# The start and the last rows of a two-layer mixer trunk: norm weight by a product with ones, another order of the first loads, splits in runs of 256, a tile apart for the last scaling

## The chip, the cores and the metric

The kernel runs on one core of a Trainium2 chip. The metric is the device time of one execution, in microseconds (us). A profile of one execution stands beside the times; its engines are called PE (TensorE, the matrix unit; PEld is its weight load), DVE (VectorE), ACT (ScalarE), POOL (GpSimd) and SP (SyncE, which here only issues DMAs).

## What is computed

256 tokens of width 1024 in float32 go through two residual layers and a last RMSNorm. The reference, cut to its frame:

```python
for layer in range(DEPTH):                       # 2
    h = rms_norm(x, norm_w[layer])               # x (1, 256, 1024)
    proj = jnp.einsum('bsd,de->bse', h, w_in[layer])     # 1024 -> 12832 columns
    ...                                          # three token mixers: SSD, sliding window, forgetting attention
    branch = jnp.einsum('bsiw,iwd->bsid', ys, w_proj[layer])
    g = jax.nn.sigmoid(gates.reshape(b, s, N_BRANCH, d) + gate_bias[layer])
    merged = jnp.sum(g * branch, axis=2)
    x = x + jnp.einsum('bsd,de->bse', merged, w_out[layer])
return rms_norm(x, final_norm_w)
```

`rms_norm` divides a row by the root of its mean square (plus 1e-6) and multiplies by a weight of 1024 entries.

## The kernel before

The tokens lie on 128 partitions in two tiles, t = 0 and t = 1. Every dense product is computed in three passes from float32 numbers split in a high and a low part of PE's fast format (`fp32r`): high by high, low by high, high by low. `split` (L261) makes both parts: ACT copies (`hi`), DVE subtracts (`lo`). A weight matrix comes in pieces; a piece is cut in parts of 512 KB, 128 by 1024, which SP loads (`load_to`, L332, six `raw` buffers), and which `feed` (L363) splits as soon as fewer than four split parts are held. `release` (L377) gives parts back and calls `feed`.

The work is a list `ops` of units: a unit is one piece by one token tile (or by one run of channels). `dense` (L278) writes the 24 matmuls of a unit: eight blocks `k` of 128 of the width, three passes each. PE's order is the list's own for the whole kernel; small jobs (transposes, attention, scan) are put between units by a clock of the program's own (`launch`, `pump`). Behind the start only PE's order is written out; the orders of the other engines are planned by the tile framework. In the start (L1139 to L1186) DVE, ACT and POOL, too, run in the order in which the program writes their instructions. Every engine runs its own in that order, and an instruction that waits holds all behind it.

The start, in words:

- SP loads x's tile 0, then the norm weight spread over 128 partitions (512 KB, `nwb`), then x's tile 1 (L161 to L163), then the weight parts.
- PE runs 30 transposes of the identity (`WARM`, L1142) that no one reads.
- For tile 0 (L1159 to L1165): squares summed, half by DVE and half by ACT; the inverse root by a power on POOL and four small DVE steps (`rsqrt`, L200); DVE scales x by root and weight in two halves of 512 columns into `h[0]`.
- `to_hT` (L270) turns four blocks of 128 by 128 on PE into one PSUM buffer, and splits the buffer at one go, 512 columns, into `hTh` and `hTl`.
- For tile 1 POOL multiplies by the weight and ACT by the root (L1167 to L1181).
- The generator `shared` (L1148) splits a weight part in halves: ACT both high halves, DVE one low half and POOL the other. It is used for parts 0 and 1 (the first piece, keys of the window attention) and for parts 2 and 3 (the second piece, its values).
- The first two units are that first piece by tile 0 and by tile 1 (`u_bkv`, L475). The first has a special order: `dense` with `after` takes blocks 0 to 3 in three passes, then blocks 4 to 7, and calls a function after every 12 matmuls (L289): `second_rows`, which turns a half of tile 1 and splits a further part.
- A unit of keys ends with `rope`: three DVE instructions on the unit's PSUM buffer (L470 to L473), then two POOL adds (L492). They stand right behind the unit in DVE's order.
- `release` at L1185 lets `feed` split the next parts; the third unit is the second piece by tile 0.

The end of the last layer, `out_end` (L993), for each tile: DVE adds the residual into `y.xn` (L996); ACT sums its squares (L997); DVE multiplies `y.xn` by -0.5 and the final weight, in place (L1001); from the sum the inverse root; DVE and ACT scale a half each (L1011, L1013) and the two halves are stored. `L8` is a tag of eight buffers of 128 by 2048 that are taken in turn.

PSUM has two kinds of buffer here: three `mm` for units, five `mx` (`pmx`) for the rest.

Of the kernel before, what the change touches and what calls it, by code (L numbers as in the profile page):

```python
# [16 lines left out]
P = 128  # L17
# [11 lines left out]
T_PP, T_SSD, T_BIAS = 1, 1, 1  # L29
N_RAW, N_SPLIT = 6, 6  # L30
AHEAD = 4
WARM = 30
VERBOSE = False


# [8 lines left out]
def hybrid_trunk(  # L44
# [53 lines left out]
    def transpose(o, a, i):  # L98
        clock["t"] += 0.109
        nc.tensor.transpose(o, a, i)  # L100
# [58 lines left out]
    x0 = T("L8", [P, 2, D])  # L159
    nwb0 = T("nwb", [P, D])  # L160
    nc.sync.dma_start(x0[:, 0, :], x2[0:P, :])  # L161
# [3 lines left out]
    make_identity(nc, ident)  # L165
    tri = T("tri", [P, P])
    nc.gpsimd.memset(tri, 1.0)
    nc.gpsimd.affine_select(out=tri, in_=tri, compare_op=ALU.is_ge, fill=0.0, base=0,
# [7 lines left out]
    ones = T("ones", [P, P])  # L176
    nc.gpsimd.memset(ones, 1.0)

    wmask = T("wmask", [P, 2 * P])
    nc.gpsimd.memset(wmask, 0.0)  # L180
# [97 lines left out]
    def dense(pt, ah, al, bh, bl, w, after=None, mid=None):  # L278


        passes = ((ah, bh), (al, bh), (ah, bl))
        if after is None:
            seq = [(k, a, b) for k in range(NK) for a, b in passes]
        else:
            seq = [(k, a, b) for k0 in (0, 4) for a, b in passes for k in range(k0, k0 + 4)]
        for i, (k, a, b) in enumerate(seq):
            mm(pt, a(k), b(k), start=(i == 0), stop=(i == len(seq) - 1))
            if after is not None:
                if i % 12 == 11:  # L289
# [111 lines left out]
        y.l = l  # L401
        layers.append(y)
    y0 = layers[0]
    y0.nwb = nwb0

    pdma = pin(nc.scalar.dma_start)

# [585 lines left out]
    def out_end(y, c, t, i, n, xo, p):  # L993
        sl = slice(c, c + n)
        with tc.high_priority():
            tt(halves(y.xn[:, t, sl]), p, halves(xo), op=ALU.add)  # L996
            sum_sq(y.xn, t, c, y.ss[t][:, i:i + 1], n)  # L997
            last = y.l + 1 == L
            nwb = fin["w"] if last else layers[y.l + 1].nwb
            if last:  # L1000
                stt(y.xn[:, t, sl], y.xn[:, t, sl], -0.5, nwb[:, sl], op0=ALU.mult, op1=ALU.mult)  # L1001
            else:
                nc.scalar.dma_start(xres[t * P:(t + 1) * P, sl], y.xn[:, t, sl])
            if i == 1:
                y.var[t] = row_var(y.ss[t], 2)
            if i == 2:
                v = y.var[t][:, 1:2]
                stt(v, y.ss[t][:, 2:3], 1.0 / D, y.var[t][:, 0:1], op0=ALU.mult, op1=ALU.add)
                r = row_rsqrt2(v)
                if last:  # L1010
                    ts(y.xn[:, t, 0:512], y.xn[:, t, 0:512], r[:, 0:1], None, op0=ALU.mult)  # L1011
                    nc.sync.dma_start(out2[t * P:(t + 1) * P, 0:512], y.xn[:, t, 0:512])
                    act(y.xn[:, t, 512:D], y.xn[:, t, 512:D], AF.Copy, scale=r[:, 0:1])  # L1013
                    nc.scalar.dma_start(out2[t * P:(t + 1) * P, 512:D], y.xn[:, t, 512:D])
# [30 lines left out]
    def op(i, *fs):  # L1045
        for f in fs:
            ops.append((i, f))

    for y in layers:
# [32 lines left out]

        if l == 0:
            k, v = cols(C_BK), cols(C_BV)
            op(k, u_bkv(y, 0, 0, [lambda j=j: second_rows(j) for j in range(2)]))
# [51 lines left out]

    ENG = mybir.EngineType
    with tc.manual_schedule(engines={ENG.PE, ENG.DVE, ENG.Activation, ENG.Pool}):  # L1139
        load_to(N_RAW)  # L1140
        warm = pmx()
        for i in range(WARM):  # L1142
            transpose(warm[:, 0:P], ident, ident)
        ss = [T("ss", [P, 4], bufs=4) for _ in range(2)]
        h = [T("L4", [P, D]) for _ in range(2)]
        y0.hTh = T("L8", [P, NK // 2, 2, 2 * P], F32R)
        y0.hTl = T("L8", [P, NK // 2, 2, 2 * P], F32R)
        def shared():  # L1148
            for _ in range(2):
                raw, hi, lo = new_part()  # L1150
                for k, sub_ in ((0, tt), (2, gtt)):
                    ks = slice(k, k + 2)
                    act(hi[:, ks, :], raw[:, ks, :], AF.Copy)  # L1153
                    sub_(lo[:, ks, :], raw[:, ks, :], hi[:, ks, :].bitcast(F32), op=ALU.subtract)  # L1154
                yield
        w0, w1 = shared(), shared()
        half = (slice(0, 512), slice(512, D))
        junk = T("L2", [P, 512])
        nc.vector.tensor_tensor_reduce(out=junk, in0=x0[:, 0, half[1]], in1=x0[:, 0, half[1]], scale=1.0,  # L1159
                                       scalar=0.0, op0=ALU.mult, op1=ALU.add, accum_out=ss[0][:, 1:2])  # L1160
        sum_sq(x0, 0, 0, ss[0][:, 0:1], 512)
        r0 = row_rstd(ss[0], 2)
        sum_sq(x0, 1, 0, ss[1][:, 0:1], 512)
        for sl in half:
            stt(h[0][:, sl], x0[:, 0, sl], r0[:, 0:1], y0.nwb[:, sl], op0=ALU.mult, op1=ALU.mult)  # L1165
        sum_sq(x0, 1, 512, ss[1][:, 1:2], 512)
        gtt(h[1][:, half[0]], x0[:, 1, half[0]], y0.nwb[:, half[0]], op=ALU.mult)  # L1167
        v1 = row_var(ss[1], 2)
        to_hT(h[0], 0, y0.hTh, y0.hTl, (0,))
        r1 = rsqrt(v1, 1)  # L1170
        next(w0)
        to_hT(h[0], 0, y0.hTh, y0.hTl, (1,))
        gtt(h[1][:, half[1]], x0[:, 1, half[1]], y0.nwb[:, half[1]], op=ALU.mult)
        def second_rows(j):
            with tc.high_priority():
                to_hT(h[1], 1, y0.hTh, y0.hTl, (j,))
            next(w1)

        act(h[1][:, half[0]], h[1][:, half[0]], AF.Copy, scale=r1[:, 0:1])
        next(w0)  # L1180
        act(h[1][:, half[1]], h[1][:, half[1]], AF.Copy, scale=r1[:, 0:1])  # L1181
        for i, f, _ in ops[:2]:
            f(pieces[i])
        pieces[0].last = True
        release(pieces[0], 2)  # L1185
        run_op(*ops[2])  # L1186
    with tc.manual_schedule(engines={ENG.PE}):
        for i, f, last in ops[3:]:
# [33 lines left out]
```

## Time and profile before

| | us |
|---|---|
| median of 3 runs | 849.24 |
| the runs | 850.91, 849.24, 848.19 |
| span of the profiled execution | 846.0 |
| PE busy in it | 833.7 |
| DVE, ACT, POOL busy | 642.3, 511.6, 105.7 |
| first weight matmul starts | 10.67 |
| third unit starts | 20.22 |
| last matmul starts | 838.84 |

The profiled execution is known by its span alone, from the first instruction to the last; the runs' times hold what lies around it as well.

How to read the profile: a row of the timeline has the start from the span's start, the time that the instruction or a merged group took, the engine, the line of the program, the operation, what it writes and reads, the shape and the count, and in brackets how long the engine stood idle before and whose end it waited for. Groups have the busy time and the mean of one in ns. A group of matmuls in plain float32 holds two records for each product in the program. Lists of waits give the sum in us, how often, and the longest.

### The profile page before, as it was taken

The page shows a single profiled execution, that of the slowest core. Times are in us where ns is not written, and L with a number is a line of the kernel's source. Part 1 is how long each engine was busy: PE and PEld are TensorE (multiplying, and loading weights), DVE is VectorE, ACT ScalarE, POOL GpSimd, SP SyncE. Part 2 cuts the span into 40 slices and gives each one's busy share as a digit, 9 for nine tenths or more (in the row PEclk, how much of TensorE's full clock was granted, in tenths as well). Part 3 has the DMA queues.
Part 4 walks back from the last instruction along what each step waited for, and adds up shares of the span by engine and source line. Part 5 has one row for each costly group of instructions (what it writes and reads, how often), then busy time and mean ns, then how long its engine had stood idle before and what let it go on. Part 6 is the DMA issues. An engine that isn't in the chain of part 4 may idle for free.

```text
span 846.0 us, 15985 instructions
## 1 busy us (share of the span) xinstructions
PE 833.7 (99%) x5964; PEld 763.4 (90%) x5964; DVE 642.3 (76%) x1403; ACT 511.6 (60%) x1004; POOL 105.7 (12%) x134
## 2 busy tenths in 40 slices
PE   8999999999999999999999999999999999999996
PEld 7989898998999998888989998899899999988896
DVE  5777997998776669656788879879968567785665
ACT  6466777665666667435555667776557667654442
POOL 6410100000140010210014001000003110121000
PEclk9999999999999999999999999999999999999999
DMA  9576565666465545748676465465755654576632
GB/s 303 160 226 197 180 199 163 197 212 184 143 188 177 181 145 189 230 147 292 206 237 218 144 204 157 145 200 182 239 172 176 174 175 152 161 236 211 212 100 76
DMA packets 126638, 158.43 MB, mean 187 GB/s; under 512 B 12784, under 2 KB 88224, under 8 KB 126560
## 3 DMA queue, kind: packets, MB, share of 16 engines
q1 hardware_dynamic: 109456, 140.79, 52.5%
q10 hardware_dynamic: 17056, 16.49, 6.3%
q8 instruction: 47, 0.77, 0.4%
q14 instruction: 31, 0.25, 0.1%
q0 software_dynamic: 48, 0.13, 0.0%
HBM read 155.22 MB, written 2.16 MB: 186 GB/s over the span
## 4 chain that ended last, share of the span: by engine, by line
PE 95%; DMA 3%; DVE 1%; ACT 0%; POOL 0%; issue 0%; SPq 0%; POOLq 0%; DVEq 0%
PE mm L96 82%; PE mx L96 9%; PE mx L100 4%; DMA raw<-in_w_in_dram 3%; DVE lo L265 0%; POOL lo L1154 0%; ACT hi L1153 0%; DVE L L470 0%; ACT L L1013 0%; DVE L L265 0%; ACT L L264 0%; POOLq L1218 0%; ACT L L215 0%; DVE L L996 0%; DVE L L1001 0%
## 5 line engine op out<-in xcount | busy, mean ns | idle before, releaser
L265 DVE TENSOR_TENSOR lo<-raw,hi 128x1024 fp32r<-128x1024 f32 x252 | 308.3, 1235 | 93.8 <-ACT hi L264 84.6
L96 PE MATMUL mm<-hi,L 128*128 128x512 f32 (+1 forms) x1344 | 373.9, 364 | 2.0 <-ACT hi L1153 1.5
L264 ACT ACTIVATE hi<-raw 128x1024 fp32r<-128x1024 f32 x252 | 263.4, 1056 | 93.5 <-PE mm L96 75.5
L96 PE MATMUL mm<-L,hi 128*128 128x256 f32 x1792 | 317.7, 278 | 0.7 <-DVE L L473 0.7
L96 PEld LDWEIGHTS mm<-L,hi 128*128 128x128 f32 x1792 | 277.7, 192 | 7.6 <-issue 3.3
L96 PEld LDWEIGHTS mm<-hi,L 128*128 128x128 f32 x1344 | 241.5, 190 | 32.5 <-issue 2.7
L96 PE MATMUL mm<-L,lo 128*128 128x256 f32 x896 | 246.4, 275 | 0.0
L96 PE MATMUL mm<-lo,L 128*128 128x512 f32 (+1 forms) x672 | 241.4, 361 | 0.6 <-POOL lo L1154 0.6
L96 PEld LDWEIGHTS mm<-L,lo 128*128 128x128 f32 x896 | 171.9, 192 | 0.2
L96 PEld LDWEIGHTS mm<-lo,L 128*128 128x128 f32 x672 | 127.3, 190 | 15.4 <-POOL lo L1154 0.8
L867 POOL TENSOR_SCALAR_AFFINE_SELECT bias<-bias 128x128 f32<-128x128 f32 x64 | 35.9, 597 | 407.5 <-DVE L L736 268.6
L561 ACT ACTIVATE pp<-pp,nm 128x128 f32<-128x128 f32 (+1 forms) x128 | 56.5, 443 | 13.5 <-DVE nm L555 13.5
L698 DVE SCALAR_TENSOR_TENSOR L<-L,vec,L 128x255 f32<-128x255 f32 (+2 forms) x96 | 46.3, 482 | 4.7 <-ACT L L695 3.4
L96 PE MATMUL mx<-L,L 128*64 128x128 f32 (+1 forms) x384 | 34.4, 314 | 0.0
L891 ACT ACTIVATE L<-L 128x512 f32<-128x512 f32 x24 | 15.1, 631 | 29.9 <-DVE L L890 29.7
L573 DVE TENSOR_SCALAR pp<-pp,rsum 128x128 f32<-128x128 f32 (+1 forms) x128 | 32.2, 316 | 0.5
L701 ACT ACTIVATE L<-L 128x256 f32<-128x256 f32 x32 | 13.3, 417 | 31.5 <-DVE L L698 25.9
L96 PEld LDWEIGHTS mx<-L,L 128*64 128x64 f32 x384 | 23.0, 136 | 9.4 <-ACT pp L561 1.3
L782 ACT ACTIVATE L<-mm 128x256 f32<-128x256 f32 x48 | 18.1, 378 | 20.8 <-PE mm L96 20.8
L590 ACT ACTIVATE L<-mx 128x512 f32<-128x512 f32 x48 | 27.0, 597 | 2.7 <-PE mx L100 2.5
L100 PE MATMUL mx<-ident,pp 128*128 128x128 f32 x192 | 26.3, 273 | 0.0
L555 DVE CUSTOM_DVE_ANT_0 pp<-mx,wmask,nsink 128x128 f32<-128x128 f32 x64 | 23.4, 412 | 1.5 <-PE mx L96 1.5
(173 smaller groups left out, 717.5 us busy)
## 6 DMA issues: line engine op xcount, KB each, us to landing
raw<-in_w_in_dram SPq DMA_DIRECT2D x200, 512.0 KB, 4.5
raw<-in_w_proj_dram SPq DMA_DIRECT2D x48, 512.0 KB, 5.5
raw<-in_w_out_dram SPq DMA_DIRECT2D x16, 512.0 KB, 4.6
L<-cumd ACTq DMA_DIRECT2D x8, 512.0 KB, 5.0
bias<-cumd ACTq DMA_DIRECT2D x16, 256.0 KB, 4.0
L<-in_gate_bias_dram ACTq DMA_DIRECT2D x12, 256.0 KB, 3.9
L<-in_x_dram SPq DMA_DIRECT2D x2, 512.0 KB, 4.9
nwb<-in_norm_w_dram SPq DMA_DIRECT2D x1, 512.0 KB, 5.3
```

What stands on the lines that cost most here:

```text
L96: nc.tensor.matmul(o, a, b, **kw)
L100: nc.tensor.transpose(o, a, i)
L264: keep(act)(hi, src, AF.Copy)
L265: keep(tt)(lo, src, hi.bitcast(F32), op=ALU.subtract)
L555: nc.vector.tensor_tensor_reduce(out=pp[:, i, sl], in0=score(p, i, b), in1=biases(p, i, b), scale=-0.125, scalar=1.0e30 if ns is None else ...
L561: act(pp[:, i, sl], pp[:, i, sl], AF.Exp, scale=-1.0, bias=nm[:, e:e + 1], accum_out=sums[:, e:e + 1])
L573: ts(pp[:, i, sl], pp[:, i, sl], rs[:, 2 * i + b:2 * i + b + 1], 0.5, op0=ALU.mult, op1=ALU.mult)
L590: act(pT, pt, AF.Copy)
L698: stt(a[:, s:S], x_[:, 0:S - s], y.vec[:, 16 * j + u:16 * j + u + 1], a[:, s:S], op0=ALU.mult, op1=ALU.add)
L782: act(halves(th), p, AF.Tanh, scale=0.5)
L867: nc.gpsimd.affine_select(out=bias[:, i, dst], in_=bias[:, i, src], compare_op=ALU.is_ge, fill=NEG, base=0, pattern=[[-1, P]], channel_mul ...
L891: act(g, g, AF.Tanh, scale=0.5)
```

## The change

It touches the start and the last rows.

- The norm weight of the first layer is no longer loaded to all partitions. One row (`nwr`, 4 KB) comes by ACT's queue, and PE multiplies a row of ones with each half of it, which leaves the weight on all 128 partitions in two `mx` buffers (`nwp`).
- SP loads the first weight part between the two tiles of x.
- The warm-up is 10 transposes, the two products, and 14 more transposes.
- x is scaled in place, in `x0`; for tile 0 and tile 1 DVE does both products, reading the weight from PSUM; the root takes one small step less.
- A turned buffer is split in two runs of 256 columns, each by ACT and then DVE.
- `dense` calls a function after every 4 matmuls of the first unit. The second half of tile 0 is turned behind the first four, the second part's split and the scaling of tile 1 are written behind the first twelve, and the turns of tile 1 behind the 16th and the 20th.
- Parts 0 and 1 are still split in halves (part 0's low halves both by POOL); parts 2 and 3 are left to `feed`, whole, behind the second unit.
- In the last layer L1001 writes to a tile of its own (`fin["y"]`), from which the last scaling and the stores go on.

```diff
-WARM = 30
+WARM = 10
+WARM2 = 14
...
+    x0 = T("L8", [P, 2, D])
+    nwr = T("L4", [1, D])
+    nc.scalar.dma_start(nwr, norm_w[0:1, :])
+    nc.sync.dma_start(x0[:, 0, :], x2[0:P, :])
...
-    nc.sync.dma_start(nwb0, norm_w[0:1, :].to_broadcast([P, D]))
-    nc.sync.dma_start(x0[:, 1, :], x2[P:S, :])
...
-                if i % 12 == 11:
-                    after[i // 12]()
+                if i % 4 == 3:
+                    after[i // 4]()
...
-                stt(y.xn[:, t, sl], y.xn[:, t, sl], -0.5, nwb[:, sl], op0=ALU.mult, op1=ALU.mult)
+                if i == 0 and t == 0:
+                    fin["y"] = T("L8", [P, 2, D])
+                stt(fin["y"][:, t, sl], y.xn[:, t, sl], -0.5, nwb[:, sl], op0=ALU.mult, op1=ALU.mult)
...
+        load_to(1)
+        nc.sync.dma_start(x0[:, 1, :], x2[P:S, :])
         load_to(N_RAW)
         warm = pmx()
         for i in range(WARM):
             transpose(warm[:, 0:P], ident, ident)
+        half = (slice(0, 512), slice(512, D))
+        nwp = [pmx() for _ in half]
+        for p, sl in zip(nwp, half):
+            mm(p, ones[0:1, :], nwr[:, sl], start=True, stop=True)
+        for i in range(WARM2):
+            transpose(warm[:, 0:P], ident, ident)
...
+        def hi_of(p, t, j, a):
+            act(y0.hTh[:, 2 * j + a, t, :], p[:, a * S:(a + 1) * S], AF.Copy)
+
+        def lo_of(p, t, j, a):
+            tt(y0.hTl[:, 2 * j + a, t, :], p[:, a * S:(a + 1) * S], y0.hTh[:, 2 * j + a, t, :].bitcast(F32),
+               op=ALU.subtract)
...
+        square(0, 1)
         sum_sq(x0, 0, 0, ss[0][:, 0:1], 512)
+        root = first_root(0)
+        tt(x0[:, 0, half[0]], x0[:, 0, half[0]], nwp[0], op=ALU.mult)
+        r = last_root(*root)
+        scaled(0, 0, r)
+        stt(x0[:, 0, half[1]], x0[:, 0, half[1]], r[:, 0:1], nwp[1], op0=ALU.mult, op1=ALU.mult)
+        split2(new_part(), (gtt, gtt))
+        p = turned(0, 0)
+        for a in range(2):
+            hi_of(p, 0, 0, a)
+            lo_of(p, 0, 0, a)
         sum_sq(x0, 1, 0, ss[1][:, 0:1], 512)
+        square(1, 1)
+        root = first_root(1)
+        tt(x0[:, 1, half[0]], x0[:, 1, half[0]], nwp[0], op=ALU.mult)
...
+        def second_part():
+            raw, hi, lo = new_part()
+            for k in (0, 2):
+                act(hi[:, k:k + 2, :], raw[:, k:k + 2, :], AF.Copy)
+            r = last_root(*root)
+            scaled(1, 0, r)
+            stt(x0[:, 1, half[1]], x0[:, 1, half[1]], r[:, 0:1], nwp[1], op0=ALU.mult, op1=ALU.mult)
+            for k, sub_ in zip((0, 2), (gtt, tt)):
+                sub_(lo[:, k:k + 2, :], raw[:, k:k + 2, :], hi[:, k:k + 2, :].bitcast(F32), op=ALU.subtract)
...
+        steps.extend([second_half, lambda: None, second_part, lambda: second_rows(0), lambda: second_rows(1),
+                      lambda: None])
+        f(w)
+        g(w)
+        w.last = True
+        release(w, 2)
         run_op(*ops[2])
```

More of the change, by code (lines that the diff above doesn't have):

```diff
@@ L1084, in hybrid_trunk @@
             k, v = cols(C_BK), cols(C_BV)
-            op(k, u_bkv(y, 0, 0, [lambda j=j: second_rows(j) for j in range(2)]))
+            steps = []
+            op(k, u_bkv(y, 0, 0, steps))
             op(k, u_bkv(y, 0, 1))
@@ L1179, in hybrid_trunk, with square @@
[L1179 to L1185, printed above, removed]
+        def square(t, h):
+            junk = T("L2", [P, 512])
+            nc.vector.tensor_tensor_reduce(out=junk, in0=x0[:, t, half[h]], in1=x0[:, t, half[h]], scale=1.0,
+                                           scalar=0.0, op0=ALU.mult, op1=ALU.add,
+                                           accum_out=ss[t][:, h:h + 1])
@@ new lines, in turned, with split2 @@
+        def turned(t, j):
+            p = pmx()
+            for k in range(4):
+                transpose(p[:, k * P:(k + 1) * P], x0[:, t, j * 512 + k * P:j * 512 + (k + 1) * P], ident)
+            return p
+        def hi_of(p, t, j, a):
[3 more added lines that the diff above has]
+               op=ALU.subtract)
+        def split2(part, subs_):
+            raw, hi, lo = part
+            for k, sub_ in zip((0, 2), subs_):
+                ks = slice(k, k + 2)
+                act(hi[:, ks, :], raw[:, ks, :], AF.Copy)
+                sub_(lo[:, ks, :], raw[:, ks, :], hi[:, ks, :].bitcast(F32), op=ALU.subtract)
```

70 lines of the change are left out of this document (32 added, 38 removed).

## The prediction

> **What bounds the kernel now.** I read the page, then TensorE's own waits, then 1 us windows over the front, then the timeline at both ends.
>
> ```profile
> span 846.0 us, 15985 instructions
> PE 833.7 (99%) x5964; PEld 763.4 (90%) x5964; DVE 642.3 (76%) x1403; ACT 511.6 (60%) x1004; POOL 105.7 (12%) x134
> ...
> PE mm L96 <- ACT hi L1153: 1.5, 1, 1.5
> ...
> PE mm L96 <- DVE L L473: 0.7, 1, 0.7
> PE mm L96 <- POOL lo L1154: 0.6, 1, 0.6
> ```
>
> TensorE (PE) is busy for 99% of the span. Of its waits the two of L1153 and L1154 belong to the start-up's split of the first weights; the one on L473 (0.7 us, at 55 us) is the only one of this size behind it. The trunk moves as one block with the moment at which PE's unbroken run begins, so only the two ends can be won. One row of the timeline and three windows (us, then busy time of PE, PEld, DVE, ACT, POOL, then the granted clock) show the front's two costs:
>
> ```profile
> 10.67 1.50 PE L96 MATMUL mm<-hi,L 128*128 128x256 f32 x8 [1.53 <-ACT hi L1153]
> ...
> 13.00:14.00 1.00, 0.98 (x5) 0.98 (x6) 0.51 (x1) 0.27 (x1) 1.00 (x1) 0.55 1.09 368
> 14.00:15.00 1.00, 1.00 (x6) 1.00 (x6) 0.00 (x0) 0.32 (x1) 1.00 (x2) 0.50 1.06 391
> 16.00:17.00 1.00, 1.00 (x8) 1.00 (x8) 1.00 (x2) 0.93 (x2) 0.00 (x0) 0.75 1.04 383
> ```
>
> PE does nothing for 1.5 us before its first weight matmuls at 10.67, and from about 13.1 (0.55 over 13 to 14) to 16.5 (0.75 over 16 to 17) its clock is halved.
>
> The execution shown has a span of 846.0 us; the median of the runs is 849.24, so 3.2 us lie around the span or between executions, and I carry them over. From no change this kernel can be told at about 0.3%, 2.5 us.
>
> **The change, part by part.** All times below are from the start of the span. The durations:
>
> ```profile
> 1.52 5.79 PE L100 MATMUL mx<-ident 128*128 128x128 f32 x30 [1.52 <-POOL ident masks.py:199]
> 5.42 0.85 PE L100 MATMUL mx<-ident 128*128 128x128 f32 x3
> 6.49 0.71 PE L100 MATMUL mx<-ident 128*128 128x128 f32 x5
> ...
> 4.33 0.69 DVE L1159 CUSTOM_DVE_ANT_0 L<-L 128x512 f32<-128x512 f32 x1 [3.40 <-DMA L<-in_x_dram]
> 5.63 0.57 POOL L203 TENSOR_TENSOR sm<-sm,mhalf 128x1 f32<-128x1 f32 x1 [1.44 <-DVE sm L220]
> 6.23 0.16 DVE L205 TENSOR_TENSOR sm<-sm 128x1 f32<-128x1 f32 x1 [0.75 <-POOL sm L203]
> 6.43 0.16 DVE L206 TENSOR_TENSOR sm<-sm,sm 128x1 f32<-128x1 f32 x1
> 7.01 1.42 DVE L1165 SCALAR_TENSOR_TENSOR L<-L,rs,nwb 128x512 f32<-128x512 f32 x2
> 7.82 1.32 PE L100 MATMUL mx<-ident,L 128*128 128x128 f32 x8 [0.51 <-DVE L L1165]
> 8.02 0.63 ACT L215 ACTIVATE L<-L 128x512 f32<-128x512 f32 x1 [2.96 <-DMA L<-in_x_dram]
> 9.86 0.69 DVE L265 TENSOR_TENSOR L<-mx,L 128x512 fp32r<-128x512 f32 x1
> 9.98 1.15 ACT L1153 ACTIVATE hi<-raw 128x512 fp32r<-128x512 f32 x2 [0.15 <-DMA raw<-in_w_in_dram]
> ...
> 23.10 0.38 ACT L485 ACTIVATE L<-mm 128x256 f32<-128x256 f32 x1 [0.24 <-PE mm L96]
> 833.99 0.48 DVE L1011 TENSOR_SCALAR L<-L,rs 128x512 f32<-128x512 f32 x1
> ...
> L96 PE MATMUL mx<-L,ones 128*128 128x128 f32 x32 | 4.9, 275 | 0.0
> L96 PE MATMUL mx<-L,bt 128*128 128x256 f32 x16 | 4.8, 380 | 0.0
> ```
>
> *Loads.* The 512 KB spread of the norm weight leaves SP's queue and one row of 4 KB goes out on ACT's; SP now issues x first half, first weight part, x second half, other parts. Each keeps a slot that a same-sized transfer had: x at 4.33 and 8.02 (its second half stays third in the queue), the first weight part in the place of the norm weight, which was in use by 7.01, the second where the first landed, 9.98. So the part that PE waited for lands about 3 us earlier, and costs nothing new. The row's own landing isn't in the trace: it lies between its issue, near 0.8, and 4.33, when all of x, 128 such rows issued at the same time, is in. I take it as there by 3.65, when PE first asks; at the late end PE's products move by 0.7.
>
> *Edits with one answer, nothing.* The ones are filled ahead of the masks on POOL (four fills and selects of the masks start a little later; none is read before the attention). ACT issues the row's transfer ahead of its first table load, and isn't needed until 4.33. The two products hold two of the five small PSUM buffers until DVE has scaled the second tile; the fourth turned block takes the buffer of the first product, last read at 11.5 by the count below. If that read slipped past 14.2 it would hold PE's last transposes.
>
> *PE before the first transpose.* Ten cold transposes 0.21 us apart (three in 0.85) run from 1.52 to 3.65. Then the two products of a row of ones with 512 columns. No row has that shape. Between 128 and 256 columns an f32 record grows from 275 to 380 ns, 0.82 ns a column, and a product is two records (16 records in the group for 8 products in the code): 2 x 512 x 0.82 = 0.84 us at full clock, 1.7 at half. The ends: 0.4 each, if one pass did, and 1.7 each, if the clock stays low through both. The 30 warm-up transposes change from 0.21 to 0.11 us apart (five in 0.71) at about 6.2, so the first product ends at 5.5, the second, half of it slow, at 6.65. Fourteen transposes at 0.11 bring PE to 8.15, where before its first real transposes began at 7.82: they lose 0.3.
>
> *DVE's chain for the first half.* Sums and the power on POOL are as before, to 6.20. The multiply by the spread weight (0.65) hides under that power if the product is there by 5.5. The root takes three small steps of 0.2 for four, the scaling 0.48 for 0.75: ready at 7.3 instead of 7.75, and PE isn't free until 8.15. The gain is lost there.
>
> *Runs of 256.* The eviction in halves starts after two transposes instead of four: ACT at 8.57 (0.38 each), DVE's subtraction at 8.97. Before, ACT had the two squares of the second tile in front of its first eviction. PE's first four matmuls start at 9.0 instead of 10.67. Then DVE, strictly in its written order, is the bound without a gap: two subtractions (one 256 wide is 0.42 long below, with the next some 0.35 behind it) to 9.7, the second tile's square 0.7, two small 0.35, the weight multiply 0.7, two subtractions 0.7, the root 0.6, the scaling 0.48, and at 13.3 PE may transpose the second tile. The scaling of its right half (0.7) and half of the second part's subtraction (0.7) end at 14.6. PE needs that last one for its final four matmuls, has done both transposes (0.45 each) and four matmuls (0.45) by then, and leaves the first unit at 15.1. POOL's share is two powers of 0.57 and three half pieces, each at most the 1.82 of a POOL row below that shares with DVE: 6.6 us between 5.6 and 14.6, hidden behind DVE's chain at nothing; the last of them would cost only if it ended past 14.6.
>
> *Second unit.* Twenty-four matmuls 0.11 apart (20.22 to 20.44 holds two, below) take 2.7 us, to 17.8; the four subtractions (14.6 to 16.0) stay ahead of it. Before, the third unit began at 20.22: 2.4 us gained.
>
> *What is late next.* The weight parts 2 and 3 were split in halves by DVE and POOL inside the front (L1154), and are no longer. They come with the release after the second unit, and in DVE's order that is behind that unit's rope, which needs PE's last matmul. The trace has the same place:
>
> ```profile
> 20.22 0.38 PE L96 MATMUL mm<-hi,L 128*128 128x256 f32 x2
> 20.44 0.28 PE L96 MATMUL mm<-lo,L 128*128 128x256 f32 x1
> ...
> 20.42 0.42 DVE L470 TENSOR_TENSOR L<-mm,rope 128x256 f32<-128x256 f32 x1 [0.34 <-PE mm L96]
> 21.16 1.22 DVE L265 TENSOR_TENSOR lo<-raw,hi 128x1024 fp32r<-128x1024 f32 x1
> 21.17 1.82 POOL L492 TENSOR_TENSOR L<-L,L 128x256 f32<-128x256 f32 x1
> 22.29 1.78 DVE L265 TENSOR_TENSOR lo<-raw,hi 128x1024 fp32r<-128x1024 f32 x1
> ```
>
> DVE waited 0.34 us there although the next split was ready. The first low half is done 2.16 us after the third unit's start (22.38 against 20.22); its third matmul needs it 0.23 in, so PE waits 2.0. The second, stretched to 1.78 beside POOL, ends 3.85 in; PE asks at 3.55: 0.35 more. Sum 2.35. The bounds are 0 (another order) and 3.
>
> *Tail.* The last product by the final weight goes to a tile of its own, so DVE needn't wait for ACT, which still reads the old one:
>
> ```profile
> 839.15 0.42 DVE L996 TENSOR_TENSOR L<-mm,L 128x256 f32<-128x256 f32 x1 [0.25 <-PE mm L96]
> 839.93 0.19 ACT L215 ACTIVATION_READ_ACCUMULATOR L<-L 128x1 f32 x1
> 840.15 0.42 DVE L1001 SCALAR_TENSOR_TENSOR L<-L,nwb 128x256 f32<-128x256 f32 x1 [0.57 <-ACT L L215]
> 840.49 0.15 DVE L1008 SCALAR_TENSOR_TENSOR sm<-ss,sm 128x1 f32<-128x1 f32 x1
> ```
>
> The variance step moves from 840.49 to 840.15: 0.34 gained. The tile takes the place of an older one last read long before, at no cost.
>
> *Sum:* -2.4 + 2.35 - 0.34 = -0.4 us; 849.24 becomes 848.8.
>
> **The rivals.** *Half clock.* In the 3.4 us before 13.1 (as long as the halved stretch), PE ran the eight matmuls of the row at 10.67 and two more, 1.1 us of work at 0.11 each, and lost half its clock. In the same stretch it would now run eighteen of this size (2.0 us): enough, I think, but the 3.4 us around the wait of the third unit hold only 1.0 to 1.5. One such stretch costs up to 1.7 us, by the windows' 0.50: -0.4 + 1.7 = +1.3, 850.5. Where the drop came, PE's longest gap was 1.5 us. The Trainium skill, "TensorE: Matmul & The Clock Gate", section "Why this matters for your kernels", asks only that gaps stay under some 3 us; by that rule no clock is lost here and the forecast stays at 848.8. The drop at 13.1 disagrees with it, so the rival keeps its chance.
>
> *The gain is kept.* If parts 2 and 3 are subtracted before the rope, the 2.35 us fall away: -2.75, 846.5; with the 0.7 us hole on L473 closed too, 845.8. For it speaks that ACT has their high halves long before; against it DVE's wait of 0.34 above.
>
> *A new hole in the trunk.* Only PE's order is written out behind the front; the other engines' is planned from a timeline that the change shifts. The one hole of today is of that kind:
>
> ```profile
> 31.47 1.33 ACTq L259 DMA_DIRECT2D dsk<-in_d_skip_dram  x2
> 50.43 1.06 ACT L264 ACTIVATE hi<-raw 128x1024 fp32r<-128x1024 f32 x1 [1.13 <-DMA raw<-in_w_in_dram]
> 51.94 1.07 ACT L264 ACTIVATE hi<-raw 128x1024 fp32r<-128x1024 f32 x1 [0.45 <-DMA raw<-in_w_in_dram]
> 55.40 0.38 PE L96 MATMUL mm<-L,hi 128*128 128x256 f32 x1 [0.73 <-DVE L L473]
> ```
>
> Parts asked for behind the d_skip load land late, DVE waits for their split and the rope behind it holds PE. Parts land 1.5 us apart there; two more caught are 3 us, and with the -0.4 that is +2.6, 851.8 and over. It decides from 2.9 us of new waiting on. Against it: DVE has two more parts to subtract behind the second unit (2.4 us) but starts 2.4 us sooner, so it frees the buffers, and the requests go out, about as before.
>
> **How the numbers follow.** Gain given back: 0.35. Half clock: 0.17. Gain kept: 0.28. New hole: 0.20. The first two are within 0.3% (0.52), the third is faster, the fourth slower. I predict the first, 848.8, by itself 847.4 to 850.2 from the stall's and the product's bounds. The range takes in the kept gain with its closed hole and the new hole's beginning: 845.8 to 851.8.
>
> **What would show it.** PE's transposes at 8.15 and matmuls at 9.0; the third unit near 17.8 with PE waiting some 2.3 us on DVE's L265 right behind; a granted clock of 1.00 from 10 to 20 us; the last L1001 beside ACT's square. I am wrong if that wait is missing, if the product is slow enough to hold DVE's multiply past 6.2, or if PE has new waits after 30 us.

## The result and the profile after

The changed kernel takes 853.34 us (median of 6 runs, 851.97 to 856.83). The kernel before takes 848.80 (6 runs, 847.80 to 852.42). The ratio is 1.0058, with a 95% interval of 1.0037 to 1.0078: slower by 4.5 us, where 848.8 and no change that can be told were forecast. The profiled execution after has a span of 851.6 and a time of 853.39. In every run that shows both, 1.7 to 1.8 us lie around the span, not 3.2; by that the execution shown of before took about 847.75 and was a quick one. The spans differ by 5.63 us for that reason, the medians by 4.5.

The page's first lines after:

```profile
span 851.6 us, 15978 instructions
PE 837.7 (98%) x5962; PEld 764.3 (90%) x5962; DVE 648.1 (76%) x1410; ACT 510.3 (60%) x1002; POOL 99.9 (12%) x131
```

TensorE's own waits in the kernel after (sum in us, how often, the longest):

```profile
PE mm L97 <- DVE lo L265: 1.6, 1, 1.6
...
PE mm L97 <- ACT hi L1230: 1.5, 1, 1.5
PE mx L101 <- issue: 0.9, 1, 0.9
PE mm L97 <- ACT L L1172: 0.8, 2, 0.5
PE mx L101 <- DVE L L939: 0.4, 1, 0.4
```

The wait on L265 is the one that the forecast put behind the third unit's start. The others of the front are new or have moved, and the one on L939 is a new hole in the trunk, at 393.6. The timeline of after shows the front up to the fourth unit:

```profile
3.85 3.77 PE L97 MATMUL mx<-L,ones 1*128 1x512 f32 x4
...
6.66 2.52 POOL L1183 TENSOR_TENSOR lo<-raw,hi 128x512 fp32r<-128x512 f32 x2 [0.29 <-ACT hi L1182]
...
7.00 0.96 DVE L1196 TENSOR_TENSOR rs<-sm,sm 128x1 f32<-128x1 f32 x1
...
7.55 3.25 PE L101 MATMUL mx<-ident 128*128 128x128 f32 x14
...
8.00 1.47 DVE L1200 TENSOR_SCALAR L<-L,rs 128x512 f32<-128x512 f32 x1
...
10.59 1.06 PE L101 MATMUL mx<-ident,L 128*128 128x128 f32 x4
...
11.69 0.38 ACT L1172 ACTIVATE L<-mx 128x256 fp32r<-128x256 f32 x1 [4.59 <-PE mx L101]
...
12.11 0.42 DVE L1175 TENSOR_TENSOR L<-mx,L 128x256 fp32r<-128x256 f32 x1 [1.99 <-ACT L L1172]
12.12 0.51 PE L97 MATMUL mm<-hi,L 128*128 128x256 f32 x2 [0.47 <-ACT L L1172]
...
12.56 0.38 ACT L1172 ACTIVATE L<-mx 128x256 fp32r<-128x256 f32 x1 [0.49 <-DVE L L1175]
12.98 0.42 DVE L1175 TENSOR_TENSOR L<-mx,L 128x256 fp32r<-128x256 f32 x1 [0.45 <-ACT L L1172]
...
16.40 1.29 POOL L1235 TENSOR_TENSOR lo<-raw,hi 128x512 fp32r<-128x512 f32 x1 [1.31 <-ACT hi L1230]
...
16.61 1.09 DVE L1196 TENSOR_TENSOR rs<-sm,sm 128x1 f32<-128x1 f32 x1
...
17.74 0.49 DVE L1200 TENSOR_SCALAR L<-L,rs 128x512 f32<-128x512 f32 x1
...
18.33 0.63 PE L101 MATMUL mx<-ident,L 128*128 128x128 f32 x4 [0.94 <-issue]
...
24.59 0.60 PE L97 MATMUL mm<-hi,L 128*128 128x256 f32 x4
24.79 0.42 DVE L469 TENSOR_TENSOR L<-mm,rope 128x256 f32<-128x256 f32 x1 [1.66 <-PE mm L97]
...
25.52 6.86 DVE L265 TENSOR_TENSOR lo<-raw,hi 128x1024 fp32r<-128x1024 f32 x5
...
26.79 0.38 PE L97 MATMUL mm<-lo,L 128*128 128x256 f32 x1 [1.60 <-DVE lo L265]
```

The two products end at 7.6 instead of 6.65, and the 14 transposes behind them run 0.22 us apart, not 0.11. PE's first real transposes come at 10.59, later than before the change (7.82). Everything of the front stands behind that:

| us from the span's start | before | forecast | after |
|---|---|---|---|
| first real transposes on PE | 7.82 | 8.15 | 10.59 |
| first weight matmul | 10.67 | 9.0 | 12.12 |
| second tile's first transposes | 13.57 | 13.3 | 18.33 |
| second unit | 17.15 | 15.1 | 21.30 |
| third unit | 20.22 | 17.8 | 24.59 |
| fourth unit | 22.90 | | 29.48 |
| last matmul | 838.84 | | 844.80 |

Where the 5.63 us of span came from: 4.37 by the third unit, 2.21 more between the third and the fourth (4.89 apart against 2.68). Before's hole of 0.73 at 55 us is gone, the new one of 0.43 stands at 393.6, and the distance at the last matmul is 5.96. The tail gives back 0.34.

### The profile page after: what moved, and what is told of

It reads as the page before. It is cut to its first block, busy times and chain, and to the rows that moved or that the text cites. A ratio compares the mean times of both kernels' runs of the same rounds, so it can differ in the third digit from the quotient of the medians.

```text
span 851.6 us, 15978 instructions
## 1 busy us (share of the span) xinstructions
PE 837.7 (98%) x5962; PEld 764.3 (90%) x5962; DVE 648.1 (76%) x1410; ACT 510.3 (60%) x1002; POOL 99.9 (12%) x131
## 5 line engine op out<-in xcount | busy, mean ns | idle before, releaser
L265 DVE TENSOR_TENSOR lo<-raw,hi 128x1024 fp32r<-128x1024 f32 x254 | 310.2, 1234 | 94.8 <-ACT hi L264 86.3
L890 ACT ACTIVATE L<-L 128x512 f32<-128x512 f32 x24 | 15.1, 631 | 30.5 <-DVE L L889 30.3
L101 PE MATMUL mx<-ident,L 128*128 128x128 f32 x152 | 23.5, 282 | 1.4 <-issue 0.9
```

The costliest lines, as they stand in the source:

```text
L265: keep(tt)(lo, src, hi.bitcast(F32), op=ALU.subtract)
L890: act(g, g, AF.Tanh, scale=0.5)
```

## The experiments

Two theories stood at first for the front. *Clock:* the products, whose weights are one row of 128, don't count as work for TensorE's clock, so all until 12 us runs at the low rate. *Chain:* DVE, ACT and POOL are the bound, by the runs of 256 and by POOL's share, and PE merely waits. The first four runs each undo one piece of the change. For each, the times are the median and the extremes of its runs, the ratio that to the kernel before on the same chip.

**e1: the product fills all 128 rows.** The weight is left out: the spread value is 1.

```diff
+    flat = T("L2", [P, 512])
+    nc.vector.memset(flat, 1.0 / P)
...
-            mm(p, ones[0:1, :], nwr[:, sl], start=True, stop=True)
+            mm(p, ones, flat, start=True, stop=True)
```

> The changed kernel, with the two products made from 128 rows (all 1/128) in place of one row; the norm weight of the first layer is thereby left out (taken as 1), all else stays. Theory (rows): a product that fills one of 128 rows does not count as work for the clock, so the clock stays halved through the products and nearly all of the 14 transposes (first full clock at 12.03 us in the changed kernel's profile). With 128 rows the full clock comes before 8.5 us, the first turned block starts at about 9.5 instead of 10.59 (DVE's scaling, which ends at 9.47, is then the bound), and the span falls by 1 to 2 us from 851.6. Rival (phase): the late clock is where the free-running window happened to lie; then full clock comes at 10 to 12 us again and the span stays within 0.5 us of 851.6.

Measured: 853.33 (852.15 to 856.09), ratio 1.0061 (1.0045 to 1.0077), span 851.67. Its timeline:

```profile
3.71 3.62 PE L97 MATMUL mx<-L,ones 128*128 128x512 f32 x4
...
7.12 1.76 PE L101 MATMUL mx<-ident 128*128 128x128 f32 x14
...
9.43 0.66 PE L101 MATMUL mx<-ident,L 128*128 128x128 f32 x4 [0.54 <-DVE L L1202]
```

Two of PE's waits in e1:

```profile
PE mx L101 <- DVE L L941: 1.0, 1, 1.0
...
PE mm L97 <- DVE L L474: 0.4, 1, 0.4
```

The same products, as long as before, but with 128 rows: the transposes behind them are quick at once (1.76 us for 14 instead of 3.25), and the trace's clock record begins, with the full clock, at 7.26 instead of 12.03. (Windows print 1.00 for the time ahead of that first entry too; there the low rate shows only in the spacing of the matmuls.) The clock theory holds. PE now waits 0.54 for DVE, so both theories have a share, one behind the other. The third unit starts at 23.00 and the fourth at 27.88, 1.6 sooner than after; yet the span is the same. Of the two waits of the second fence the one of 0.4, at 60.4, is new, and the one of 1.0, at 393.5, was 0.4 in after: the trunk took the 1.6 back. That wasn't expected, and led to e7.

**e2: runs of 512 again** for the turned buffers, as before the change.

```diff
-        for a in range(2):
-            hi_of(p, 0, 0, a)
-            lo_of(p, 0, 0, a)
+        both(p, 0, 0)      # split(...) of the whole 512 columns; likewise for the other three
```

> The changed kernel with each turned block split at one go of 512 columns, as before the change, instead of two runs of 256. Theory (one engine at a time on a buffer): ACT's second run waited for DVE's first (0.49 us each time), so two runs take 1.73 us for a block against 1.26 for one go; three of the four blocks lie on the path, so the third unit starts about 1.2 us earlier than 24.59 and the span falls by about 1.2. Rival (runs help): PE starts its first matmuls later by 0.4 and the span rises by as much.

Measured: 851.91 (850.82 to 856.60), ratio 1.0042 (1.0024 to 1.0060), span 849.10. Its timeline:

```profile
11.69 0.60 ACT L264 ACTIVATE L<-mx 128x512 fp32r<-128x512 f32 x1 [4.47 <-PE mx L101]
12.32 0.69 DVE L265 TENSOR_TENSOR L<-mx,L 128x512 fp32r<-128x512 f32 x1 [2.06 <-ACT L L264]
...
17.07 0.63 PE L101 MATMUL mx<-ident,L 128*128 128x128 f32 x4 [1.32 <-issue]
```

A block takes 1.3 us from ACT's start to DVE's end (11.69 to 13.01), where the two runs of after take 1.7 (11.69 to 13.40): ACT's second run waits 0.49 for DVE's first, on the same PSUM buffer. The second tile's transposes come 1.26 sooner, the third unit (21.94) 2.65, where 1.2 was forecast. In the profiled execution the clock isn't halved in the front, in the one of after it is, from 18.85. The windows of the 3.4 us ahead of that moment (us, busy time of PE, PEld, DVE, ACT, POOL, granted clock, DMA share, GB/s) in after:

```profile
15.40:18.80 3.40, 1.47 (x9) 1.09 (x10) 2.86 (x6) 1.42 (x3) 1.29 (x1) 1.00 0.06 23
```

The same in e2:

```profile
15.40:18.80 3.40, 2.08 (x18) 1.91 (x19) 3.16 (x7) 0.76 (x2) 0.65 (x1) 1.00 0.07 26
```

PE worked 1.47 us there in after and 2.08 in e2. Part of e2's gain is thus the clock's, and how much can't be told from one execution.

**e3: parts 2 and 3 split before the second unit,** whole, so ahead of its rope.

```diff
         f(w)
+        for _ in range(2):
+            raw, hi, lo = new_part()
+            split(hi, lo, raw)
         g(w)
```

> The changed kernel with the weight parts 2 and 3 split ahead of the second unit, so that DVE's subtractions stand before that unit's rope instead of behind it. Theory (order): the third unit no longer waits (1.60 us and a short second wait), the step from the third unit's start to the fourth's falls from 4.9 us to 2.7, and the span falls by about 2.0 us. Rival: DVE is full there, the rope comes late instead and PE waits elsewhere; the span stays within 0.5.

Measured: 852.68 (851.18 to 856.32), ratio 1.0054 (1.0028 to 1.0080), span 850.78. Its timeline:

```profile
22.87 2.90 DVE L265 TENSOR_TENSOR lo<-raw,hi 128x1024 fp32r<-128x1024 f32 x2
24.59 0.61 PE L97 MATMUL mm<-hi,L 128*128 128x256 f32 x4
...
25.70 0.41 DVE L469 TENSOR_TENSOR L<-mm,rope 128x256 f32<-128x256 f32 x1
```

Two of PE's waits in e3:

```profile
PE mx L101 <- DVE L L939: 0.8, 1, 0.8
...
PE mm L97 <- DVE L L472: 0.4, 1, 0.4
```

The subtractions now stand ahead of the rope, the third unit starts at the same 24.59, and the fourth at 27.27 instead of 29.48: the wait of 2.2 us is gone. The span fell by 0.86 only, where 2.0 was forecast. Most of the rest went into two holes, as in e1: a new one of 0.4 at 59.8, and the one at 392.7, which grew from 0.4 to 0.8.

**e4: DVE makes the first part's low halves,** not POOL.

```diff
-        split2(new_part(), (gtt, gtt))
+        split2(new_part(), (tt, tt))
```

> The changed kernel with both low halves of weight part 0 subtracted by DVE, behind its scaling of the first tile, instead of by POOL. Theory (shared way to the buffers): POOL's two subtractions held DVE's one-column step (0.96 us instead of 0.16) and its scaling (1.47 instead of 0.48); without them the scaling ends near 7.7 instead of 9.47. As PE is not free before 10.59 this alone gains nothing: span within 0.5 of 851.6, a little worse (+0.5 to +1.3) if DVE's two extra subtractions delay the second tile. Rival (DVE sets the front): span falls by 1 or more.

Measured: 853.68 (852.43 to 858.42), ratio 1.0064 (1.0040 to 1.0088), span 852.02; third unit at 24.57, no gain. In after DVE's small step takes 0.96 and the scaling 1.47 beside POOL's L1183. The same scaling takes 0.49 at 17.74, and in e4 the two take 0.16 and 0.49, so that the first tile is ready at 7.68 instead of 9.47. But PE isn't free before 10.59 anyway, so alone this delay costs nothing.

**e5: three mends at once, with the weight kept.** The row lies in a tile of 128 rows of which 127 are zero, and the product has 128 rows; 16 transposes stand ahead of it and 8 behind; with e2's and e3's edits.

```diff
-WARM = 10
-WARM2 = 14
+WARM = 16
+WARM2 = 8
-    nwr = T("L4", [1, D])
-    nc.scalar.dma_start(nwr, norm_w[0:1, :])
+    nwr = T("L4", [P, D])
+    nc.vector.memset(nwr, 0.0)
+    nc.scalar.dma_start(nwr[0:1, :], norm_w[0:1, :])
...
-            mm(p, ones[0:1, :], nwr[:, sl], start=True, stop=True)
+            mm(p, ones, nwr[:, sl], start=True, stop=True)
```

> The changed kernel with three of its parts altered together: the row of the norm weight lies in a tile of 128 rows whose other rows are zero, so that the product fills all rows (16 warm-up transposes ahead of it, 8 behind); blocks split at one go of 512; parts 2 and 3 split ahead of the second unit. Theory (the terms add): full clock before 8.5 us, third unit near 21.8 us, fourth near 24.5 (22.9 in the kernel before), span 847 to 848.5, so still 1 to 2.5 behind the 846.0 of before, because DVE's own chain for the second tile is what remains. If only values other than zero count for the clock, full clock comes after 10 us. Rival (the front sets all): span at or under 845.7.

Measured: 850.74 (848.72 to 854.06), ratio 1.0019 (1.0001 to 1.0037), span 848.91, third and fourth unit at 22.76 and 25.52. Its timeline:

```profile
6.22 3.62 PE L97 MATMUL mx<-L,ones 128*128 128x512 f32 x4 [1.02 <-DMA L<-in_norm_w_dram]
...
8.30 0.69 DVE L1210 TENSOR_TENSOR L<-L,mx 128x512 f32<-128x512 f32 x1 [2.73 <-PE mx L97]
...
9.67 1.04 PE L101 MATMUL mx<-ident 128*128 128x128 f32 x8
```

The row's transfer waits for the fill, lands at 6.2, and PE and DVE stand for it. The product is nearly all that PE did from 6.2 to 9.6, and the full clock came at 9.56 (9.76 in e6), later than the 8.5 that was forecast, as the row was late. By these runs rows count even where 127 of them hold zeros. The fourth unit comes a microsecond behind its forecast of 24.5.

**e6: e5, and e4's edit.**

```diff
-        split2(new_part(), (gtt, gtt))
+        split2(new_part(), (tt, tt))
```

> As e5_three, with the low halves of part 0 on DVE behind the scaling instead of on POOL. Theory: DVE's scaling of the first tile ends near 7.7 instead of 9.4, the first turned block starts near 8.1 instead of 9.4, third unit near 21, fourth near 23.7; span about 0.8 under e5_three. Rival (DVE full): the two subtractions come back later in DVE's chain, the second tile's first turned block starts no earlier than in e5_three, and the span is the same within 0.4.

Measured: 849.49 (847.17 to 856.24), ratio 1.0018 (0.9992 to 1.0044); fourth unit at 25.74. No gain over e5 in the front (25.52): DVE waits for the late product there. The profiled execution is one of the long ones, with a span of 851.93: behind the front lie a hole of 2.5 us that ends at 392.39 and half a clock from 392.06 to 395.47.

**e7: the kernel before, with d_skip loaded otherwise.** In e1 and e3 what the front won was lost in holes near 60 and 393 us. Each lies behind the load of a layer's `d_skip`, which spreads 16 numbers over the partitions as two strided loads. Here one row of 16 is spread, and two small DVE steps sort it.

```diff
-        for half in range(2):
-            src = d_skip[l:l + 1, :].rearrange("o (j two) -> two o j", two=2)[half]
-            pdma(y.dsk[64 * half:64 * half + 64, :], src.to_broadcast([64, NK]))
+        y.d16 = T("d16", [P, 16], bufs=2)
+        pdma(y.d16, d_skip[l:l + 1, :].to_broadcast([P, 16]))
...
+        for half in range(2):
+            hp = slice(64 * half, 64 * half + 64)
+            pin(ts)(y.dsk[hp, :], y.d16.rearrange("p (j two) -> p two j", two=2)[hp, half, :], 1.0, None, op0=ALU.mult)
```

> The kernel before, with d_skip loaded as one row of 16 spread over 128 partitions and sorted to its place by two small DVE steps, in place of two loads of single numbers (1024 packets of 4 bytes); the result is the reference's. Theory (small packets): the two loads held all transfers behind them (no traffic from 36 to 45 us, 8 to 15 us to landing); without them the weight parts asked for at 33 to 45 us land in 4 to 7 us, PE's 0.73 us wait at 55 us goes, span 845.3. Rival: the pause comes from elsewhere (the requests themselves wait), the landing times stay and the span too (within 0.3).

Measured: 846.09 (846.01 to 846.66, 10 runs), ratio 0.9965 (0.9952 to 0.9977), span 844.80. The page's line on packets, of before and of e7:

```profile
DMA packets 126638, 158.43 MB, mean 187 GB/s; under 512 B 12784, under 2 KB 88224, under 8 KB 126560
```

```profile
DMA packets 124814, 158.44 MB, mean 188 GB/s; under 512 B 10960, under 2 KB 86400, under 8 KB 124736
```

A window behind the first of these loads (columns as above), of before and of e7:

```profile
38.00:40.00 2.00, 2.00 (x13) 1.76 (x12) 2.00 (x5) 0.18 (x1) 1.27 (x1) 1.00 0.05 0
```

```profile
38.00:40.00 2.00, 2.00 (x13) 1.76 (x12) 2.00 (x7) 0.36 (x2) 1.51 (x1) 1.00 1.11 375
```

The landing of the weight parts that SP issues between 20 and 70 us, of before and of e7:

```profile
DMA to landing us min/median/max: 3.4/5.4/15.0
```

```profile
DMA to landing us min/median/max: 4.0/4.8/7.0
```

The strided loads, four of 2 KB in the whole kernel, make 1,824 packets more. Behind the first two, issued at 31.47, nothing moves for a while (0 GB/s in this window and in all from 36 to 44 us), and weight parts land up to 15 us after their issue instead of 7. Without it no hole over 0.25 us is left behind 15 us, and the runs lie within 0.65 us of each other, where the kernel before's 31 runs beside them spread over 6.7 (846.69 to 853.38).

**e8: the kernel before with the tail alone.**

```diff
-                stt(y.xn[:, t, sl], y.xn[:, t, sl], -0.5, nwb[:, sl], op0=ALU.mult, op1=ALU.mult)
+                if i == 0 and t == 0:
+                    fin["y"] = T("L8", [P, 2, D])
+                stt(fin["y"][:, t, sl], y.xn[:, t, sl], -0.5, nwb[:, sl], op0=ALU.mult, op1=ALU.mult)
```

> The kernel before, with the last rows scaled into a tile apart and nothing else of the change. Theory: the last L1001 product starts beside ACT's square, the variance step comes 0.34 us sooner, span 845.7; too little for the times to tell. Rival (the new tile has to wait for its place): span over 846.2.

Measured: 847.80 (846.64 to 849.68), ratio 0.9981 (0.9964 to 0.9997). From the last matmul to the end of the span 6.83 us, against 7.17 before: 0.34, as forecast. The ratio's 1.6 us are more than that. Part of it may be the clock, which isn't halved in this execution's front (fourth unit at 21.76, against 22.90 before); that isn't shown for the other runs.

**e9: before, with the tail and e7's load.** The edits are those of e7 and e8.

> The kernel before, with d_skip loaded as one row (as in e7_dsk) and the last rows scaled into a tile apart (as in e8_tail). Theory (independent): span 844.8 - 0.34 = 844.4, times near 845.8 and as close together as those of e7_dsk (0.65 us). Rival: the times spread over some 5 us again, if the close times of e7_dsk were chance.

Measured: 845.94 (845.75 to 846.25), ratio 0.9973 (0.9962 to 0.9983), span 844.18. It beats both kernels, and the tail's part is on top of e7's within what the runs can tell (846.09 for e7).

**e10: the changed kernel with e7's load.** The edit is e7's.

> The changed kernel with d_skip loaded as one row, as in e7_dsk. Theory (the holes behind d_skip's loads give and take): without them the front's loss reaches the end whole: fourth unit at 29.4 against 22.7 in e7_dsk, so 6.7 - 0.34 = 6.3 us over e7_dsk's 844.8, span 851.1. Rival (no such holes): the same gain of 1.2 to 2.7 us as e7_dsk brought, span under 850.5.

Measured: 852.67 (852.63 to 852.85), ratio 1.0053 (1.0036 to 1.0070), span 851.14. Against e7, with the noise of the trunk out of both, the change costs 851.14 - 844.80 = 6.3 us. At the fourth unit the two are 6.79 apart (29.50 against 22.71); the tail's 0.34 comes off that. Against e9, which has the tail too and ran on the same chip, the medians are 6.7 us apart.

**e11: e10 with the edits of e1 to e4 together.** The weight is left out, as in e1.

> The changed kernel with d_skip as one row and four alterations of the front: product from 128 rows of 1/128 (the norm weight of the first layer is left out), blocks split at one go, parts 2 and 3 split ahead of the second unit, part 0's low halves on DVE. Theory (terms add, with the product there early): full clock before 8.5, first turned block near 8, third unit near 20.5, fourth near 23.2; span 845.0, level with e7_dsk within 0.8. Rival (DVE's chain bounds): DVE has both products of the second tile and one more low half; third unit at 22 or later, span 846.4 or more.

Measured: 845.37 (845.08 to 845.76), ratio 0.9961 (0.9943 to 0.9979), span 844.02; third and fourth unit at 19.52 and 22.35, the clock full from 7.09 and not halved in the front. Its timeline:

```profile
6.87 0.16 DVE L1204 TENSOR_TENSOR rs<-sm,sm 128x1 f32<-128x1 f32 x1
...
7.06 0.48 DVE L1208 TENSOR_SCALAR L<-L,rs 128x512 f32<-128x512 f32 x1
...
8.64 0.60 PE L101 MATMUL mx<-ident,L 128*128 128x128 f32 x4
```

All four together bring the fourth unit from 29.50 to 22.35, level with e7 (22.71). But e7's front has one halved stretch and e11's none; e8, with the front of before and no halved stretch, has its fourth unit at 21.76. So between them the four hold the loss but for some 0.6 us. With PE free earlier, POOL's share counts as well: the small step and the scaling are back at 0.16 and 0.48, and the first transposes come at 8.64, where e1 with POOL's share had 9.43.

**e12: e10 without the product.** The weight is spread by a load again, second in SP's queue, ahead of the first weight part, and 30 transposes stand in one run.

```diff
-WARM = 10
-WARM2 = 14
+WARM = 30
+    nwb0 = T("nwb", [P, D])
     nc.sync.dma_start(x0[:, 0, :], x2[0:P, :])
+    nc.sync.dma_start(nwb0, norm_w[0:1, :].to_broadcast([P, D]))
...
-        nwp = [pmx() for _ in half]
-        for p, sl in zip(nwp, half):
-            mm(p, ones[0:1, :], nwr[:, sl], start=True, stop=True)
-        for i in range(WARM2):
-            transpose(warm[:, 0:P], ident, ident)
+        nwp = [nwb0[:, sl] for sl in half]
```

> The changed kernel with d_skip as one row and the product undone: the norm weight comes by DMA as in the kernel before, second in SP's queue, and the warm-up is the 30 transposes in one run; the rest of the change stays. Theory (rows): full clock near 6 to 8, PE free at 7.3, first turned block set by DVE (weight in at 6.5, POOL in its way) near 9.4; third unit near 23, 1.6 us ahead of e10_after_dsk; span 849.5. Rival (the product is not the cost): third unit at 24 or later, span within 0.5 of e10_after_dsk.

Measured: 851.05 (849.48 to 851.83), ratio 1.0029 (1.0017 to 1.0041), span 847.77; first real transposes at 8.33, third unit at 21.12, fourth at 26.08. In the two profiled executions the product, with its time and its cold clock, costs 3.4 us, where 1.6 was forecast. But e12's is the quickest of its six: the others take 1.3 to 2.4 us longer, for a cause that no trace shows, and the medians of e10 and e12 are 1.6 apart. So the price lies somewhere between the two. e1, which took the cold clock alone out, showed 1.6 at the third unit. Of the rest, 26.08 against e7's 22.71, the wait behind the third unit is 2.3 (4.96 from third to fourth unit, against e7's 2.67). That the other 1.1 are the runs of 256 and POOL's share is argued from the rows, not shown by a run of its own.

From the second tile's turn to the second unit e12, at full clock and still in runs of 256, takes 1.88:

```profile
16.39 0.66 PE L100 MATMUL mx<-ident,L 128*128 128x128 f32 x4 [0.89 <-DVE L L1197]
...
18.27 0.40 PE L96 MATMUL mm<-hi,L 128*128 128x256 f32 x2
```

## Why the prediction was wrong

The third unit was forecast at 17.8 and started at 24.59. The 6.8 us come apart by the prediction's own steps:

- **"PE before the first transpose"** failed: 2.44. The products end 0.9 later than forecast; they take 1.9 each, beyond the upper end of 1.7. The transposes behind them take 3.04 until PE turns the first block, not 1.5. The step took the clock's rise, at about 6.2, from a stretch of transposes of 128 rows, and carried it to one in which PE spends 3.8 of 9.3 us on one-row products. e1 showed that the rise depends on them (7.26 with 128 rows, 12.03 with one).
- **"Runs of 256"** failed, in two places. From the first real transposes to the first weight matmul 1.53 instead of 0.85 (0.68 of the 6.8): the transposes are still cold, 1.06 us for four, and ACT starts at 11.69, behind the fourth of them (over at 11.65), where the forecast started it behind the second. In e1, with quick transposes, it is 1.13. From there to the second tile's turn 6.21 instead of 4.3 (1.91). "With the next some 0.35 behind it" was wrong: DVE's second run starts 0.87 after its first, since ACT's second copy waits for DVE's subtraction on the same buffer. The Trainium skill, "PSUM — Partial Sum Buffer", section "PSUM bank collisions raise a hardware error", says that two engines may not touch the same part of a PSUM bank at once, reads included, and that the compiler puts a dependency between them. The trace agrees, with ACT's 0.49 us behind DVE; e2 takes that wait out and wins 1.26 by the second tile's turn; PE's wait for ACT's copy of the second part (L1230) falls from 1.5 to 0.3.
- **POOL "hidden behind DVE's chain at nothing"** failed: POOL's pieces stretch DVE's own steps. In the first tile (1.47 for 0.48) e4 shows that this is covered as long as PE is late, e11 that it isn't once PE is early. In the second tile it lies on the path: beside POOL's L1235 DVE's step of the root takes 1.09 at 16.61, for 0.16, and the scaling and the second tile's transposes come right behind it. By the rows that is 0.9 of the 1.91 above. No run takes this piece from POOL.
- **"Second unit"**: 3.29 instead of 2.7 (0.59 of the 6.8), its beginning at half clock. The stretch ahead of it, from the second tile's turn, took 2.97 instead of 1.8 (1.17), most of it at half clock; e12's 1.88 at full clock shows that this is the clock and not the runs of 256.
- **"What is late next"** was right: 2.35 forecast, 2.21 measured, on the L265 behind the second unit's rope, and e3 takes it away by the order alone. Its first part was a little smaller than forecast (1.60 of waiting for 2.0), as PE stops behind four matmuls, not two. The rival in which the gain is kept was right in its mechanism, but e3's saved wait was 0.86 at the end of the span.
- **"Tail"** was right: 0.34 forecast and measured, in after and in e8.
- **"Loads"** held: POOL subtracts the first part from 6.66 on, so it was in by then (forecast: about 7.0), and the products start at 3.85 without a wait for the row.
- **"The trunk moves as one block"** held only to within a microsecond or two. It moves with the front, but the holes behind the d_skip loads grow or shrink with it. In e1, 1.6 us won at the fourth unit were lost there. The rival of a new hole in the trunk saw the mechanism (parts behind the d_skip load land late); in after it is worth 0.43 of new waiting, far from the 2.9 us from which it was to decide.
- **Half clock**: the forecast of a full clock from 10 to 20 failed. The rival feared a halving around the third unit's wait; it came at 18.85, ahead of the second unit, in a stretch in which PE had worked 1.47 of 3.4 us, as it had come before at 13.1. Against the forecast it cost the 1.17 and a part of the 0.59 above. As before had such a stretch too, it explains little of the difference between the two kernels.

Windows of after show that stretch; PE's clock goes from 0.93 over 18 to 19 to 0.50, and rises again over 22 to 23 (0.87):

```profile
18.00:19.00 1.00, 0.67 (x6) 0.70 (x7) 1.00 (x3) 0.00 (x1) 0.00 (x0) 0.93 0.00 0
19.00:20.00 1.00, 1.00 (x6) 1.00 (x6) 0.84 (x2) 0.51 (x2) 0.00 (x0) 0.50 0.00 0
...
22.00:23.00 1.00, 1.00 (x9) 1.00 (x9) 1.00 (x4) 1.00 (x2) 0.00 (x0) 0.87 1.29 244
```

The forecast's sum had -2.4 for the front, where +4.37 was measured. The wait (+2.21) and the tail (-0.34) were as forecast; the trunk's holes and small shifts make the remaining -0.6. The band of 847.4 to 850.2 doesn't come out of the bounds that it names: a stall between 0 and 3 alone makes 846.5 to 849.5. What stays open: how much of e2's gain is the clock's, and why the other runs of e12 are longer than the one profiled. A row that is there early and fills 128 rows wasn't tried; e1 leaves the weight out, and e5's row comes late.

## What to carry to other kernels

Price a new kind of instruction at the clock that it leaves behind it, not only at its own length: a warm-up that is replaced by other work may stop being one. Before a buffer is read in smaller pieces by two engines, look for a dependency between those engines on that buffer: the pieces may alternate instead of overlapping. And before small changes of a front are weighed by their runs, find the holes of the trunk that answer to a shift: here loads of 2 KB hid part of what each mend of the front gave.

## What the runs showed of the hardware

**A product of one row doesn't warm the clock.** PE was busy without a gap from 3.85 to 10.8 in after, and the full clock came at 12.03 (11.50 to 12.27 in the other runs with one-row products). With 128 rows it came at 7.26 and 7.09, and in e5, with 127 of the rows zero, at 9.56 for products that began at 6.22. The Trainium skill, "TensorE: Matmul & The Clock Gate", section "What's actually happening", has the clock follow how busy PE was over some 3.4 us. The trace agrees for products with all rows; for products of one row it doesn't, as 3.77 us of them, with transposes ahead and behind, didn't raise it.

**The clock falls on little work, without a long idle stretch.** A window of before ahead of its drop at 13.10:

```profile
9.70:13.10 3.40, 1.79 (x11) 1.39 (x11) 2.79 (x9) 3.25 (x7) 2.44 (x3) 1.00 1.10 349
```

PE worked 1.79 us of 3.4 there, with no gap over 1.53, and 1.47 ahead of after's drop; e2's 2.08 brought none. The halved stretches that ended within the front lasted 3.41 each. Busy time alone doesn't decide: e7's drop at 13.15 came behind 2.01 us, while e12's 1.74 us from 21.29 to 24.70 brought none. The count of matmuls does, in these traces. Cut each front into steps of 3.41 us from the moment of the full clock, and take the steps at full clock that begin before 26 us. Behind each of the eleven in which 5 to 12 matmuls or transposes began (0.11 us each at full clock) came half clock, and behind none of those with 13 or more. With 12 and 13 side by side this is a rule of fourteen traces and these shapes, and no more.

**A load of few bytes can hold all others.** Two loads of 2 KB left 36 to 44 us without traffic, and without the strided loads run times that had spread over 6.7 us agreed to 0.65. It is not the only cause of spread: e12, without these loads, still spreads over 2.4.
